# A hybrid encoder block on one core: squares on ScalarE, sums and the sine's product on VectorE, a third weight piece split early, new durations in the list

## The chip, the cores and the metric

The kernel runs on one core of a Trainium2 chip. The metric is the device time of one execution in microseconds, as the median of several executions. A core has five engines with a queue of instructions each, worked off in order: PE (TensorE, matmuls and transposes), DVE (VectorE), ACT (ScalarE), POOL (GpSimd) and SP (SyncE, which here only issues transfers). They wait for one another by semaphores. Data lie in DRAM, in SBUF (128 partitions) and in PSUM, where matmuls write.

## What is computed

One layer of an encoder with two kinds of heads, on a prompt of 512 rows and a sample of 256 rows, of width 2048, with shared weights. The reference, cut:

```
h = rmsnorm(x, ln_mix_g); z = h @ w_in            # 2048 -> 1024 fourier | 1024 q | 256 k | 256 v
of = fourier_mix(zf, w_fourier)                   # real part of a 2-D DFT per group of 128 channels, then 128x128
q, k = rope(q), rope(k)
s = q.k / 8, masked to |qpos - kpos| <= 128       # 16 heads, 4 kv heads, blocks of 128 queries
m = max(max(s), sink); p = exp(s - m)
p = p / (sum(p) + exp(sink - m)); oa = p @ v
x = x + concat(rmsnorm(of, g1), rmsnorm(oa, g2)) @ w_out
x = x + relu(rmsnorm(x, ln_mlp_g) @ w_up)**2 @ w_down   # 2048 -> 8192 -> 2048
y = rmsnorm(x, ln_final_g)
```

All is float32. A matmul that must keep that precision is made of three: both operands are split into a high and a low half in a shorter format, and high x high, high x low and low x high are summed.

## The kernel before, in words

The 768 rows are NM = 6 blocks m of 128 (0 to 3 prompt, 4 and 5 sample). The stages follow each other on PE: input projection (pz, L542, to 388 us), attention together with the Fourier half of the output projection (388 to 611 us), the attention half of the output projection (611 to 768 us), up-projection (pu, L1034, to 1693 us) and down-projection (pd, L1315, to 2590 us).

**Weight pieces.** A weight is loaded in pieces of 512 KB (`wload`, two raw buffers), and each piece is split: high half on ACT (L168), low half on DVE (L182), into one of four buffers `wh` and `wl`. The output projection has 32 pieces i: half 0 (Fourier rows) and half 1 (attention rows), in each four column strips n of 512, four pieces per strip. Pieces of half 1 carry a gain (L166 on ACT, L177 on DVE, two instructions each). The input projection is a loop of 36 pieces; callables put down with `after(piece, fn)` are run behind a piece, or in the middle of it (at piece - 0.5). So the first pieces of the output projection are loaded and split under the last input pieces.

**Attention.** There are 24 units u, one for each block b of 128 queries and each kv head g (four heads each). Blocks at the ends see 2 blocks of keys, those between see 3. A unit's steps: load the rotated, split queries (`load_q`, SP); for g = 3 instead load unrotated ones and rotate here (`rotate_q`: the product with the sine on POOL, L488; with the cosine on DVE, L490; their sum on DVE, L492; split on ACT L497 and DVE L500); scores s on PE (L584); maxima on DVE (L595, then L606 and L609); exponentials on ACT (L619, L614); row sum and its reciprocal on DVE (L625, L626); the normaliser p <- p * rs on POOL (L630, four steps, one for each head); transposes t of p on PE (L638, four per block of keys, each needs all heads' normalised p of its rows); their split into th (ACT, L644) and tl (DVE, L647); products with v on PE (o, L655); `take` copies o on ACT (L662); `put` stores its two halves by SP (L668).

**Fourier half of the output projection.** 24 slots (n, m) of 8 steps with three matmuls (pm, L739); a step needs its piece's low half. ACT takes a slot's result (xc, L752), SP stores it (y1, L755). These matmuls are what PE has to do while a unit's chain runs through the other engines.

**Attention's output.** When the four units of a block m are stored, SP loads it back (`oa_load`, L686) and POOL adds the second half in an accumulating load (L688). ACT and DVE split it (`oa_part`, L696 and L698), then `oa_square` squares both halves in place (L705) and adds them (L707), on POOL, and DVE sums over channels (`oa_reduce`, L712, into sr).

**The order of all this** is not left to a scheduler. Each step is a job: engine, assumed duration, due time, the jobs it needs, and a time `wait` behind its end until its result can be used. `in_turn(hop, slack)` plays the list through: it takes again and again the job that can start first on its engine (among equals the one due first), and the starting times give the order in which the code is emitted, which is the order in each engine's queue. A result is usable at end + wait + hop; for a job on PE other than a pm step, `slack` is added, so transposes, scores and products with v are put that much behind the assumed moment at which they could run, and pm steps fill the place.

**Attention half of the output projection.** For each strip n and each pair of blocks (mp, mp + 3): SP loads rows of x into yp (L943), POOL adds the stored first half in an accumulating load (L944), 8 steps of 6 matmuls run (pm, L739), for n = 0 the sums sr give the factor r (power on POOL, L99), DVE forms r * pm + yp (L962), and the result is stored. Its transposes (`x1_transpose`, ptx, L132) are made later, in step 3 of the next pair's matmuls; DVE and ACT turn them into factors for the up-projection.

Of the kernel before, what the change touches and what calls it, by code (L numbers as in the profile page):

```python
# [14 lines left out]
AF = mybir.ActivationFunctionType  # L15
ALU = mybir.AluOpType
# [24 lines left out]
def hybrid_encoder(ctx: ExitStack, tc: tile.TileContext, a: dict):  # L41
# [150 lines left out]
    with ExitStack() as ph:  # L192
# [292 lines left out]
        def rotate_q(u, step):  # L485
            x, y = state[u]["x"], state[u]["y"]
            if step == 0:
                nc.gpsimd.tensor_tensor(out=y, in0=y, in1=table(u, "sinr"), op=ALU.mult)  # L488
            elif step == 1:
                nc.vector.tensor_tensor(out=x, in0=x, in1=table(u, "cosr"), op=ALU.mult)  # L490
            else:
                nc.vector.tensor_tensor(out=x, in0=x, in1=y, op=ALU.add)  # L492
# [30 lines left out]
        for u in range(2):  # L523
            after(32.5 + u, lambda u=u: load_q(u))
        for i in range(2):
            after(32.5 + i, lambda i=i: (out_load(i), out_split(i)))
# [173 lines left out]
    def oa_square(m, step):  # L700

        x, y = oar[m, 0], oar[m, 1]
        if step < 2:
            z = (x, y)[step]
            nc.gpsimd.tensor_tensor(out=z[:], in0=z[:], in1=z[:], op=ALU.mult)  # L705
        else:
            nc.gpsimd.tensor_tensor(out=y[:], in0=y[:], in1=x[:], op=ALU.add)  # L707

# [88 lines left out]

    for i in range(2, 22):
        half, n, j = out_seq[i]
# [21 lines left out]
    for u in range(len(units)):  # L821
# [4 lines left out]
        if u >= 2:  # L826
            job(("q", u), SP, 0.5, t0 - 8, lambda u=u: load_q(u), ("s", u - 3, 3), ("<", ("q", u - 1)), start=8 if g == 3 else -1e9, wait=4.5)
        if g == 3:
            job(("r0", u), POOL, 1.2, t0 - 6, lambda u=u: rotate_q(u, 0), ("q", u))
            job(("r1", u), DVE, 0.62, t0 - 6, lambda u=u: rotate_q(u, 1), ("q", u))  # L830
            job(("r2", u), DVE, 0.62, t0 - 5, lambda u=u: rotate_q(u, 2), ("r0", u), ("r1", u))
            job(("q0", u), ACT, 0.56, t0 - 4, lambda u=u: split_q(u, 0), ("r2", u))
            job(("q1", u), DVE, 0.75, t0 - 3, lambda u=u: split_q(u, 1), ("q0", u))
# [21 lines left out]
        for h in range(4):  # L855
            job(("n", u, h), POOL, 0.6 if wide else 0.48, t0 + 5, lambda u=u, h=h: normalize(u, h), ("rs", u))
        for kb in range(nb):
# [14 lines left out]
        job(("o", u), ACT, 0.5, t0 + 11, lambda u=u: take(u), ("pv", u, nb - 1), ("put", u - 2))  # L872
        job(("put", u), SP, 0.5, t0 + 12, lambda u=u: put(u), ("o", u), wait=4)

    for m in range(NM):
        due = SLOT * (18 + m) + 4
        job(("a0", m), SP, 1.6, due, lambda m=m: oa_load(m, 0), *(("put", 4 * m + g) for g in range(4)), ("or", m - 2), wait=4)
        job(("a1", m), POOL, 2.4, due, lambda m=m: oa_load(m, 1), ("a0", m), wait=6)
        for i in range(2):
            job(("ph", m, i), ACT, 0.62, due + 5, lambda m=m, i=i: oa_part(m, i, 0), ("a1", m), ("mm", 3, m - 1, 7), ("ph", m, i - 1))  # L880
            job(("pl", m, i), DVE, 0.65, due + 6, lambda m=m, i=i: oa_part(m, i, 1), ("ph", m, i))
        for i in range(3):
            job(("sq", m, i), POOL, 1.2, due + 9, lambda m=m, i=i: oa_square(m, i), *(("pl", m, x) for x in ((i,) if i < 2 else (0, 1))), ("sq", m, i - 1))
        job(("or", m), DVE, 1.0, due + 12, lambda m=m: oa_reduce(m), ("sq", m, 2))

    with tc.manual_schedule(engines=by_hand):
        for key in in_turn(0.05, 0.4):
            jobs[key][3]()
# [41 lines left out]
    with tc.tile_pool(name="pp4", bufs=1, space=PSUM, reuse_waits="tile") as pp:  # L930
        pending, half = [], 0
        for n in range(4):
# [4 lines left out]
            for mp in range(3):  # L937
# [10 lines left out]
                def step(k):  # L948
                    if k == 3 and pending:
                        pt = pp.tile([P, 2, 512], F32, tag="pt", name="ptx", bufs=1)  # L950
                        x1_transpose(pt, *pending[0])
                        x1_factors(pt, *pending.pop(0)[:2])
# [569 lines left out]
```

## Time and profile before

| | before |
|---|---|
| median of 3 runs | 2618.87 us (2618.65 to 2619.86) |
| profiled execution | 2620.49 us |
| span of the profile | 2618.7 us |
| mean granted clock of TensorE | 0.998 |
| PE busy | 2588.1 us (99%) |
| DVE busy | 1700.7 us (65%) |
| ACT busy | 1042.4 us (40%) |
| POOL busy | 270.5 us (10%) |

The span runs from the first to the last instruction; the profiled execution's own time is 1.8 us longer. A row of the timeline has the start, the duration, the engine, the line, the operation with its names (out <- in), the shape, and how often; in square brackets stands how long the engine was idle before and what released it. A group (of the view by lines) gives count, busy time and mean duration in ns, then the idle time ahead and its releasers. A row of waits has the waiting instruction, what it waited for, the total, the number and the longest. A row of the chain has start, duration, what ran. A row of windows gives the stretch, its length, the busy time of PE, PEld (weight loads), DVE, ACT and POOL with counts, the granted clock, the DMA engines' share and GB/s.

### The profile page before, as it was taken

How to read it: one execution, taken by the hardware profiler on the slowest of the kernel's cores; microseconds unless marked ns; L12 is line 12 of the kernel's file. 1: busy time of each engine (PE TensorE's matmuls, PEld its weight loads, DVE VectorE, ACT ScalarE, POOL GpSimd, SP SyncE). 2: the span in 40 equal slices, each digit the busy share in tenths (PEclk: the TensorE clock that was granted, in tenths of full speed). 3: DMA queues.
4: the chain of work that ended last, by engine and by line, in shares of the span. 5: the costliest groups of instructions: out<-in, count | busy, mean ns of one | idle time of the engine just before them, and what ended most of it. 6: DMA issues, size and time to landing. Idle time of an engine off the chain costs nothing.

```text
span 2618.7 us, 34937 instructions
## 1 busy us (share of the span) xinstructions
PE 2588.1 (99%) x13556; PEld 2364.2 (90%) x13556; DVE 1700.7 (65%) x2073; ACT 1042.4 (40%) x1494; POOL 270.5 (10%) x381
## 2 busy tenths in 40 slices
PE   8999999999999999999999999999999999999998
PEld 8999997887889999999999999988888888888886
DVE  4344546665655655555777787767776765777677
ACT  6233316663333333333454445433333333333335
POOL 1011213434110111000000000020000000000000
PEclk9999999999999999999999999999999999999999
DMA  8333577547774554448666666585553672555364
GB/s 295 115 117 127 163 233 207 150 131 184 203 233 143 171 182 160 176 169 305 209 221 218 219 229 221 195 350 179 179 162 110 210 241 81 177 177 162 99 209 147
DMA packets 278982, 488.23 MB, mean 186 GB/s; under 512 B 21216, under 2 KB 171488, under 8 KB 277792
## 3 DMA queue, kind: packets, MB, share of 16 engines
q1 hardware_dynamic: 202240, 329.91, 39.2%
q10 hardware_dynamic: 54576, 96.58, 9.6%
q0 software_dynamic: 22000, 59.52, 8.2%
q8 instruction: 106, 1.74, 0.3%
q14 instruction: 60, 0.49, 0.1%
HBM read 359.30 MB, written 126.62 MB: 186 GB/s over the span
## 4 chain that ended last, share of the span: by engine, by line
PE 95%; DVE 2%; POOL 1%; ACT 1%; issue 1%; DMA 1%; ACTq 0%; POOLq 0%; SPq 0%; DVEq 0%
PE pu L1034 36%; PE pd L1315 34%; PE pz L542 11%; PE pm L739 8%; PE pv L222 1%; PE o L655 1%; PE s L584 1%; PE t L638 1%; PE pa L359 1%; PE pe L380 0%; PE ptx L132 0%; POOL p L630 0%; DVE wl L182 0%; DMA yp<-in_x_sample 0%; DMA raw<-in_w_out 0%
## 5 line engine op out<-in xcount | busy, mean ns | idle before, releaser
L1034 PE MATMUL pu<-xf,wh 128*128 128x384 f32 x3328 | 848.4, 336 | 0.0
L1034 PEld LDWEIGHTS pu<-xf,wh 128*128 128x128 f32 x3328 | 600.7, 188 | 1.9 <-ACT o L1052 1.1
L1034 PE MATMUL pu<-xf,wl 128*128 128x384 f32 x1664 | 559.1, 336 | 0.0
L1315 PE MATMUL pd<-wh,sh 128*128 128x512 f32 x1320 | 513.5, 389 | 0.0
L1315 PE MATMUL pd<-wl,sh 128*128 128x512 f32 x1320 | 513.5, 389 | 0.0
L1315 PE MATMUL pd<-wh,sl 128*128 128x512 f32 x1320 | 513.5, 389 | 0.0
L1292 ACT ACTIVATE wh<-rd 128x1024 fp32r<-128x1024 f32 x200 | 202.3, 1054 | 524.0 <-PE pd L1315 416.7
L1302 DVE TENSOR_TENSOR wl<-rd,wh 128x1024 fp32r<-128x1024 f32 x200 | 236.3, 1222 | 230.4 <-ACT wh L1292 229.7
L1014 ACT ACTIVATE wh<-ur 128x1024 fp32r<-128x1024 f32 x160 | 169.9, 1062 | 374.6 <-PE pu L1034 207.7
L1034 PEld LDWEIGHTS pu<-xf,wl 128*128 128x128 f32 x1664 | 312.8, 188 | 0.0
L1315 PEld LDWEIGHTS pd<-wl,sh 128*128 128x128 f32 x1320 | 247.8, 188 | 51.6
L1315 PEld LDWEIGHTS pd<-wh,sh 128*128 128x128 f32 x1320 | 247.7, 188 | 51.4
L1315 PEld LDWEIGHTS pd<-wh,sl 128*128 128x128 f32 x1320 | 247.7, 188 | 51.3
L1020 DVE TENSOR_TENSOR wl<-ur,wh 128x1024 fp32r<-128x1024 f32 x160 | 195.6, 1223 | 81.1 <-ACT wh L1014 81.1
L1055 DVE TENSOR_TENSOR o<-pu,o 128x768 f32<-128x768 f32 x160 | 153.0, 956 | 118.4 <-PE pu L1034 114.7
L542 PE MATMUL pz<-hh,wh 128*128 128x384 f32 x576 | 147.3, 336 | 0.0
L542 PE MATMUL pz<-hh,wl 128*128 128x384 f32 x576 | 146.3, 334 | 0.0
L542 PE MATMUL pz<-hl,wh 128*128 128x384 f32 x576 | 146.1, 334 | 0.0
L1285 DVE TENSOR_TENSOR rd<-rd 128x1024 f32<-128x1024 f32 x112 | 131.9, 1220 | 0.0
L1014 ACT ACTIVATE wh<-sx 128x1024 fp32r<-128x1024 f32 x64 | 67.9, 1062 | 127.7 <-PE pu L1034 96.7
L1305 DVE TENSOR_TENSOR sl<-sr,sh 128x768 fp32r<-128x768 f32 x110 | 104.7, 952 | 0.0
L542 PEld LDWEIGHTS pz<-hh,wl 128*128 128x128 f32 x576 | 103.9, 188 | 0.3 <-DVE wl L68 0.3
(210 smaller groups left out, 3489.1 us busy)
## 6 DMA issues: line engine op xcount, KB each, us to landing
rd<-in_w_down SPq DMA_DIRECT2D x176, 512.0 KB, 5.3
ur<-in_w_up SPq DMA_DIRECT2D x128, 512.0 KB, 3.9
sr<-sd SPq DMA_DIRECT2D x94, 384.0 KB, 5.5
pd<-o ACTq DMA_DIRECT2D x64, 384.0 KB, 2.3
o<-pd POOLq DMA_DIRECT2D x64, 384.0 KB, 6.1
sd<-sm ACTq DMA_DIRECT2D x60, 384.0 KB, 2.7
raw<-in_w_in SPq DMA_DIRECT2D x36, 512.0 KB, 3.6
raw<-in_w_out SPq DMA_DIRECT2D x32, 512.0 KB, 5.0
```

Of the source, the lines that this page charges most:

```text
L222: nc.tensor.matmul(pv[m][:, :256], l[j][:, i, m * P : (m + 1) * P], wv[j][r][:, i, :], start=(k == 0 and n == 0), stop=(k == NK - 1 and n ...
L542: nc.tensor.matmul(ps[c][s][:, :HALF], w[:, i, cs], h[j][:, i, s * HALF : (s + 1) * HALF], start=first and n == 0, stop=last and n == 2,)
L739: nc.tensor.matmul(ps[:], l(k), w[:, k % 2, :], start=(k == 0 and n == 0), stop=(k == 7 and n == 2))
L1014: nc.scalar.activation(wh[:], raw[:], AF.Copy)
L1020: nc.vector.tensor_tensor(out=wl[:], in0=raw[:], in1=f32(wh[:]), op=ALU.subtract)
L1034: nc.tensor.matmul(ps[:, t, :HALF], w[:, i, t * P : (t + 1) * P], xb[:, o, i, :], start=(s == first_of[bank] and i == 0 and n == 0), stop= ...
L1055: nc.vector.tensor_tensor(out=o, in0=src, in1=o, op=ALU.add)
L1285: add = lambda x, y, op: nc.vector.tensor_tensor(out=x[:], in0=x[:], in1=y[:], op=op)
L1292: nc.scalar.activation(wh[:], t[:], AF.Copy)
L1302: nc.vector.tensor_tensor(out=wl[:], in0=t[:], in1=f32(wh[:]), op=ALU.subtract)
L1305: nc.vector.tensor_tensor(out=sl[:], in0=sr[:], in1=f32(sh[:]), op=ALU.subtract)
L1315: nc.tensor.matmul(ps[m][:, ns], l[:, q, ts], w[:, ns], start=(j == 0 and q == 0 and t == 0), stop=(j == HP // 2 - 1 and q == 1 and t == 2),)
```

## The change

Six edits. The sine's product goes from POOL to DVE. The third piece of the output weight (i = 2) is loaded and split under the last input piece, not by the list. The two squares go from POOL to ACT, their sum to DVE. In the list, durations are set anew (query loads and stores 0.5 to 1.2, accumulating loads 2.4 to 3.6, the moved steps as on their new engines) and the first unit's normaliser gets a wait of 1.2. The slack of PE's jobs other than pm goes from 0.4 to 1.0. And the transposes of the pairs of strip n = 0 in the second half are made in step 6 of the next pair, not in step 3.

```
--- before.py
+++ after.py
@@ -485,7 +485,7 @@
         def rotate_q(u, step):
             x, y = state[u]["x"], state[u]["y"]
             if step == 0:
-                nc.gpsimd.tensor_tensor(out=y, in0=y, in1=table(u, "sinr"), op=ALU.mult)
+                nc.vector.tensor_tensor(out=y, in0=y, in1=table(u, "sinr"), op=ALU.mult)
             elif step == 1:
                 nc.vector.tensor_tensor(out=x, in0=x, in1=table(u, "cosr"), op=ALU.mult)
             else:
@@ -522,7 +522,7 @@
             after(23 + i // 2 if i < 4 else 25 + (i - 4) * 10 // 12 if i < 12 else 32 + (i - 12), fn)
         for u in range(2):
             after(32.5 + u, lambda u=u: load_q(u))
-        for i in range(2):
+        for i in range(3):
             after(32.5 + i, lambda i=i: (out_load(i), out_split(i)))
         for m in range(NM):
             after(0.5 + m // 2 * 0.5, lambda m=m: row_scale(m))
@@ -702,9 +702,9 @@
         x, y = oar[m, 0], oar[m, 1]
         if step < 2:
             z = (x, y)[step]
-            nc.gpsimd.tensor_tensor(out=z[:], in0=z[:], in1=z[:], op=ALU.mult)
+            nc.scalar.activation(z[:], z[:], AF.Square)
         else:
-            nc.gpsimd.tensor_tensor(out=y[:], in0=y[:], in1=x[:], op=ALU.add)
+            nc.vector.tensor_tensor(out=y[:], in0=y[:], in1=x[:], op=ALU.add)
 
     def oa_reduce(m):
 
@@ -795,7 +795,7 @@
     for m in range(NM):
         job(("of", m), SP, 3.0, SLOT * m - 20, lambda m=m: load_of(m), start=-22 if m < 2 else SLOT * m - 20, wait=4)
 
-    for i in range(2, 22):
+    for i in range(3, 22):
         half, n, j = out_seq[i]
         need = 6 * SLOT * (n + 4 * half) + 1.4 * j
         last = ("mm", out_seq[i - 4][1], NM - 1, 2 * out_seq[i - 4][2] + 1) if i >= 4 else None
@@ -824,9 +824,9 @@
         wide = nb == 3
         heads = [(h,) for h in range(4)] if wide else [(0, 1), (2, 3)]
         if u >= 2:
-            job(("q", u), SP, 0.5, t0 - 8, lambda u=u: load_q(u), ("s", u - 3, 3), ("<", ("q", u - 1)), start=8 if g == 3 else -1e9, wait=4.5)
+            job(("q", u), SP, 1.2, t0 - 8, lambda u=u: load_q(u), ("s", u - 3, 3), ("<", ("q", u - 1)), start=8 if g == 3 else -1e9, wait=4.5)
         if g == 3:
-            job(("r0", u), POOL, 1.2, t0 - 6, lambda u=u: rotate_q(u, 0), ("q", u))
+            job(("r0", u), DVE, 0.62, t0 - 6, lambda u=u: rotate_q(u, 0), ("q", u))
             job(("r1", u), DVE, 0.62, t0 - 6, lambda u=u: rotate_q(u, 1), ("q", u))
             job(("r2", u), DVE, 0.62, t0 - 5, lambda u=u: rotate_q(u, 2), ("r0", u), ("r1", u))
             job(("q0", u), ACT, 0.56, t0 - 4, lambda u=u: split_q(u, 0), ("r2", u))
@@ -853,7 +853,7 @@
             )
         job(("rs", u), DVE, 0.28, t0 + 5, lambda u=u: row_sum(u), *(("e", u, h) for h in range(5)))
         for h in range(4):
-            job(("n", u, h), POOL, 0.6 if wide else 0.48, t0 + 5, lambda u=u, h=h: normalize(u, h), ("rs", u))
+            job(("n", u, h), POOL, 0.6 if wide else 0.48, t0 + 5, lambda u=u, h=h: normalize(u, h), ("rs", u), wait=0.1 if u else 1.2)
         for kb in range(nb):
             one = turns[-1] if turns else (-1, 0)
             two = turns[-2] if len(turns) > 1 else (-1, 0)
@@ -870,21 +870,21 @@
                 ("l", u, kb), ("pv", u, kb - 1), ("o", u - 1), wait=0.2,
             )
         job(("o", u), ACT, 0.5, t0 + 11, lambda u=u: take(u), ("pv", u, nb - 1), ("put", u - 2))
-        job(("put", u), SP, 0.5, t0 + 12, lambda u=u: put(u), ("o", u), wait=4)
+        job(("put", u), SP, 1.2, t0 + 12, lambda u=u: put(u), ("o", u), wait=4)
 
     for m in range(NM):
         due = SLOT * (18 + m) + 4
         job(("a0", m), SP, 1.6, due, lambda m=m: oa_load(m, 0), *(("put", 4 * m + g) for g in range(4)), ("or", m - 2), wait=4)
-        job(("a1", m), POOL, 2.4, due, lambda m=m: oa_load(m, 1), ("a0", m), wait=6)
+        job(("a1", m), POOL, 3.6, due, lambda m=m: oa_load(m, 1), ("a0", m), wait=6)
         for i in range(2):
             job(("ph", m, i), ACT, 0.62, due + 5, lambda m=m, i=i: oa_part(m, i, 0), ("a1", m), ("mm", 3, m - 1, 7), ("ph", m, i - 1))
             job(("pl", m, i), DVE, 0.65, due + 6, lambda m=m, i=i: oa_part(m, i, 1), ("ph", m, i))
         for i in range(3):
-            job(("sq", m, i), POOL, 1.2, due + 9, lambda m=m, i=i: oa_square(m, i), *(("pl", m, x) for x in ((i,) if i < 2 else (0, 1))), ("sq", m, i - 1))
+            job(("sq", m, i), DVE if i == 2 else ACT, 0.68, due + 9, lambda m=m, i=i: oa_square(m, i), *(("pl", m, x) for x in ((i,) if i < 2 else (0, 1))), ("sq", m, i - 1))
         job(("or", m), DVE, 1.0, due + 12, lambda m=m: oa_reduce(m), ("sq", m, 2))
 
     with tc.manual_schedule(engines=by_hand):
-        for key in in_turn(0.05, 0.4):
+        for key in in_turn(0.05, 1.0):
             jobs[key][3]()
     att.close()
     kctx.close()
@@ -946,7 +946,7 @@
                     outs.append((ps, lambda k, m=m: oa[m][0][:, k, :], lambda k, m=m: oa[m][1][:, k, :]))
 
                 def step(k):
-                    if k == 3 and pending:
+                    if pending and k == (6 if pending[0][0] == 0 else 3):
                         pt = pp.tile([P, 2, 512], F32, tag="pt", name="ptx", bufs=1)
                         x1_transpose(pt, *pending[0])
                         x1_factors(pt, *pending.pop(0)[:2])
```

What moves by it, at three places. First DVE at the end of the input projection and the start of attention. L68 is the split of an input piece, L182 the low half of an output piece, L554 takes a finished result of the input projection (zs), L595 is a row maximum of unit 0 and then of unit 1 (one instruction and the reading of its result). A row with + stands in the kernel after, with - in the one before:

```order
 L427 TENSOR_TENSOR rx<-rx,ry 128x384
+L68 TENSOR_TENSOR wl<-raw,wh 128x1024
 L71 SCALAR_TENSOR_TENSOR rl<-rx,rh 128x384
-L68 TENSOR_TENSOR wl<-raw,wh 128x1024
+L182 TENSOR_TENSOR wl<-raw,wh 128x1024
 L554 TENSOR_TENSOR zs<-pz,rb 128x384 x4
+L595 ISA s,mx<-s,mask,sink 128x256
+L595 ISA mx 128x1
```

The third piece's low half now stands ahead of the last results of the input projection, and unit 0's first maxima (three, of which the first is shown) stand ahead of the fourth piece's low half instead of behind it.

Second DVE at unit 3's rotation, after only. L647 splits unit 0's transposes, L488, L490, L492 and L500 are unit 3's rotation and split, L625 and L626 are unit 1's row sum:

```order
+L647 TENSOR_TENSOR tl<-t,th 128x512 x2
+L488 TENSOR_TENSOR ry<-ry,sinr 64x512
+L490 TENSOR_TENSOR rx<-rx,cosr 64x512
+L625 TENSOR_TENSOR rs<-rs,es 128x4
+L626 RECIPROCAL rs<-rs 128x4
+L492 TENSOR_TENSOR rx<-rx,ry 64x512
+L500 SCALAR_TENSOR_TENSOR qs<-rx,qs 64x512
```

The sine's product, which waits for a load, now has unit 1's row sum behind it in DVE's queue; on POOL it had a normaliser behind it.

Third POOL through the first three blocks. L630 is the normaliser, L688 an accumulating load of a block of attention's output, L705 and L707 squares and sum:

```order
-L630 TENSOR_SCALAR p<-p,rs 128x256 x4
-L488 TENSOR_TENSOR ry<-ry,sinr 64x512
-L630 TENSOR_SCALAR p<-p,rs 128x256 x12
+L630 TENSOR_SCALAR p<-p,rs 128x256 x16
 L630 TENSOR_SCALAR p<-p,rs 128x384 x4
-L488 TENSOR_TENSOR ry<-ry,sinr 64x512
 L688 DMA oar<-oadl_93 128x4x128 x2
-L630 TENSOR_SCALAR p<-p,rs 128x384 x8
-L705 TENSOR_TENSOR oar<-oar 128x512 x2
-L707 TENSOR_TENSOR oar<-oar 128x512
```

POOL's queue keeps the normaliser and the accumulating loads. Further on, the third block's accumulating load moves from ahead of unit 14's normaliser to behind it. On PE, 27 pm matmuls follow unit 0's scores in both kernels; then come four of unit 1's score matmuls and unit 0's first transposes before, and all eight of unit 1's scores, three more pm matmuls and then the transposes after.

More of the change, by code (lines that the diff above doesn't have):

```diff
@@ L487, in rotate_q @@
             if step == 0:
-                nc.gpsimd.tensor_tensor(out=y, in0=y, in1=table(u, "sinr"), op=ALU.mult)
+                nc.vector.tensor_tensor(out=y, in0=y, in1=table(u, "sinr"), op=ALU.mult)
             elif step == 1:
@@ L524, in hybrid_encoder @@
             after(32.5 + u, lambda u=u: load_q(u))
-        for i in range(2):
+        for i in range(3):
             after(32.5 + i, lambda i=i: (out_load(i), out_split(i)))
@@ L704, in oa_square @@
             z = (x, y)[step]
-            nc.gpsimd.tensor_tensor(out=z[:], in0=z[:], in1=z[:], op=ALU.mult)
+            nc.scalar.activation(z[:], z[:], AF.Square)
         else:
-            nc.gpsimd.tensor_tensor(out=y[:], in0=y[:], in1=x[:], op=ALU.add)
+            nc.vector.tensor_tensor(out=y[:], in0=y[:], in1=x[:], op=ALU.add)
     def oa_reduce(m):
@@ L796, in hybrid_encoder @@
         job(("of", m), SP, 3.0, SLOT * m - 20, lambda m=m: load_of(m), start=-22 if m < 2 else SLOT * m - 20, wait=4)
-    for i in range(2, 22):
+    for i in range(3, 22):
         half, n, j = out_seq[i]
@@ L826, in hybrid_encoder @@
         if u >= 2:
-            job(("q", u), SP, 0.5, t0 - 8, lambda u=u: load_q(u), ("s", u - 3, 3), ("<", ("q", u - 1)), start=8 if g == 3 else -1e9, wait=4.5)
+            job(("q", u), SP, 1.2, t0 - 8, lambda u=u: load_q(u), ("s", u - 3, 3), ("<", ("q", u - 1)), start=8 if g == 3 else -1e9, wait=4.5)
         if g == 3:
-            job(("r0", u), POOL, 1.2, t0 - 6, lambda u=u: rotate_q(u, 0), ("q", u))
+            job(("r0", u), DVE, 0.62, t0 - 6, lambda u=u: rotate_q(u, 0), ("q", u))
             job(("r1", u), DVE, 0.62, t0 - 6, lambda u=u: rotate_q(u, 1), ("q", u))
@@ L855, in hybrid_encoder @@
         for h in range(4):
-            job(("n", u, h), POOL, 0.6 if wide else 0.48, t0 + 5, lambda u=u, h=h: normalize(u, h), ("rs", u))
+            job(("n", u, h), POOL, 0.6 if wide else 0.48, t0 + 5, lambda u=u, h=h: normalize(u, h), ("rs", u), wait=0.1 if u else 1.2)
         for kb in range(nb):
@@ L872, in hybrid_encoder @@
         job(("o", u), ACT, 0.5, t0 + 11, lambda u=u: take(u), ("pv", u, nb - 1), ("put", u - 2))
-        job(("put", u), SP, 0.5, t0 + 12, lambda u=u: put(u), ("o", u), wait=4)
+        job(("put", u), SP, 1.2, t0 + 12, lambda u=u: put(u), ("o", u), wait=4)
     for m in range(NM):
@@ L877, in hybrid_encoder @@
         job(("a0", m), SP, 1.6, due, lambda m=m: oa_load(m, 0), *(("put", 4 * m + g) for g in range(4)), ("or", m - 2), wait=4)
-        job(("a1", m), POOL, 2.4, due, lambda m=m: oa_load(m, 1), ("a0", m), wait=6)
+        job(("a1", m), POOL, 3.6, due, lambda m=m: oa_load(m, 1), ("a0", m), wait=6)
         for i in range(2):
@@ L882, in hybrid_encoder @@
         for i in range(3):
-            job(("sq", m, i), POOL, 1.2, due + 9, lambda m=m, i=i: oa_square(m, i), *(("pl", m, x) for x in ((i,) if i < 2 else (0, 1))), ("sq", m, i - 1))
+            job(("sq", m, i), DVE if i == 2 else ACT, 0.68, due + 9, lambda m=m, i=i: oa_square(m, i), *(("pl", m, x) for x in ((i,) if i < 2 else (0, 1))), ("sq", m, i - 1))
         job(("or", m), DVE, 1.0, due + 12, lambda m=m: oa_reduce(m), ("sq", m, 2))
     with tc.manual_schedule(engines=by_hand):
-        for key in in_turn(0.05, 0.4):
+        for key in in_turn(0.05, 1.0):
             jobs[key][3]()
@@ L948, in step @@
                 def step(k):
-                    if k == 3 and pending:
+                    if pending and k == (6 if pending[0][0] == 0 else 3):
                         pt = pp.tile([P, 2, 512], F32, tag="pt", name="ptx", bufs=1)
```

## The prediction

> **What bounds the kernel now.** I read the page first, then PE's waits from 385 to 640 us, then PE's timeline, the chain and the windows at the places that these named.
>
> ```profile
> PE 2588.1 (99%) x13556; PEld 2364.2 (90%) x13556; DVE 1700.7 (65%) x2073; ACT 1042.4 (40%) x1494; POOL 270.5 (10%) x381
> ```
>
> TensorE is busy for 99% of the span, and the change takes no matmul away. So all that it can win is time in which PE waits or runs slowly. Nearly all of that lies in the attention stage (388 to 611 us) and in the first slots of the attention half of the out-projection (611 to 640 us). The view of PE's waits there, with the total, the number and the longest:
>
> ```profile
> PE ptx L132 <- DVE yp L962: 2.8, 1, 2.8
> PE t L638 <- POOL p L630: 1.9, 3, 1.0
> PE pm L739 <- DVE wl L177: 1.5, 1, 1.5
> PE pm L739 <- DVE wl L182: 1.5, 2, 0.8
> PE o L655 <- DVE tl L647: 0.6, 1, 0.6
> PE s L584 <- ACT p L619: 0.4, 1, 0.4
> PE pm L739 <- ACT wh L168: 0.3, 1, 0.3
> ```
>
> They sum to 9.0 us, and this counts too little in two ways. A matmul's modelled end lies behind the next one's usual start, so each wait costs about 0.16 us more than its idle figure. And a group of eight transposes that is paced by the normaliser, block by block, shows as busy. PE's timeline, the first stalls and a healthy group of eight:
>
> ```profile
> 394.21 0.50 PE L739 MATMUL pm<-wl,ofh 128*128 128x512 f32 x1 [0.73 <-DVE wl L182]
> 397.84 2.13 PE L638 MATMUL t<-ident,p 128*128 128x128 f32 x8 [1.01 <-POOL p L630]
> 409.25 1.04 PE L638 MATMUL t<-ident,p 128*128 128x128 f32 x8
> ```
>
> I therefore took the losses from PE's starts: each interval less the usual one of its kind (pm 0.23 us, one transpose 0.11, a score of 256 columns 0.12). That gives three sums: start 4.9 us (waits 3.2, and 1.7 by the clock, below), middle 8.3, tail 4.85.
>
> The clock. Behind that first stall six matmuls of one line take 2.56 us by the chain, where the same six take 1.38 later; the window (us, busy PE, PEld, DVE, ACT, POOL, then the granted clock, DMA share, GB/s) shows why:
>
> ```profile
> 400.78 2.56 PE pm L739 x6
> 410.28 1.38 PE pm L739 x6
> ```
>
> ```profile
> 400.00:403.00 3.00, 3.00 (x10) 2.52 (x10) 2.32 (x7) 1.06 (x4) 0.00 (x0) 0.50 1.07 266
> ```
>
> The clock stood at 0.50 for 3.4 us, which costs 1.7.
>
> **The start: third weight piece split early, and the list's order.** Once the in-projection ends, ACT and DVE split pieces three and four one after the other, and the row maxima stand behind them. DVE, ACT, POOL:
>
> ```profile
> 390.40 1.23 DVE L182 TENSOR_TENSOR wl<-raw,wh 128x1024 fp32r<-128x1024 f32 x1 [1.55 <-ACT wh L168]
> 392.94 1.22 DVE L182 TENSOR_TENSOR wl<-raw,wh 128x1024 fp32r<-128x1024 f32 x1
> ```
>
> ```profile
> 391.62 1.06 ACT L168 ACTIVATE wh<-raw 128x1024 fp32r<-128x1024 f32 x1 [1.26 <-DMA raw<-in_w_out]
> ```
>
> ```profile
> 397.31 1.84 POOL L630 TENSOR_SCALAR p<-p,rs 128x256 f32<-128x256 f32 x4 [20.66 <-ACT xc L752]
> ```
>
> With the third piece done under the in-projection (its load is issued right behind the last input weight, its buffers are those of an earlier input piece), the fourth takes the third's place: low half done at 390.40 + 1.22, about 391.6. PE needs it at 394.21 less the stall of 0.89, that is 393.3, so this wait goes. Three of unit 0's maxima now come ahead of the fourth piece, so DVE's path to the row sums loses 1.23 + 1.22 and small gaps, 2.54 in my replay with these durations; the normaliser begins at 397.31 - 2.54 = 394.8 and its four steps of 0.46 end at 396.6. PE now has eight scores and three matmuls more where four scores stood, and comes to the first transposes at 397.0: no wait, by 0.4. Transposes done at 397.9 instead of 399.7, with 4 x 0.12 + 3 x 0.23 = 1.16 of other work done besides: 3.0 us. If the cover fails, it fails by the fourth piece's load (it was waited for, 1.26, in the row above) and costs at most the old 3.2. The clock's 1.7 I let go with the stall that it follows, for the profile; the profiled run is 2620.49 against a median of 2618.87, 1.62 more, so the timed runs may not have it. Start: 4.7 against the profile, 3.0 to 4.9.
>
> By the Trainium skill, "TensorE: Matmul & The Clock Gate", section "HAM oscillation — how this bites in real kernels", a slowed clock follows a gap in PE's work of more than about 3.4 us; here the gaps ahead of it are 0.73 and 1.01 us, so the row disagrees, and by that rule alone the 1.7 would come from something that this change does not touch: 3.0 for the start.
>
> **The middle: products and squares off POOL.** The stalls, one for each kind, and what POOL did ahead of the first:
>
> ```profile
> 517.55 2.63 POOL L688 DMA_DIRECT2D oar<-oadl  x2 [6.76 <-DMA oar<-oadh]
> ```
>
> ```profile
> 520.75 2.09 PE L638 MATMUL t<-ident,p 128*128 128x128 f32 x8 [0.51 <-POOL p L630]
> 566.25 1.39 PE L638 MATMUL t<-ident,p 128*128 128x128 f32 x8
> 570.55 0.50 PE L739 MATMUL pm<-wl,ofh 128*128 128x512 f32 x1 [0.76 <-DVE wl L182]
> 583.38 2.04 PE L638 MATMUL t<-ident,p 128*128 128x128 f32 x8
> 593.74 1.88 PE L638 MATMUL t<-ident,p 128*128 128x128 f32 x8
> ```
>
> Against a healthy 1.04 these groups lose 1.05 + 0.35 + 1.00 + 0.84, with the idle 0.51 and 0.76 before them 4.5; the other 3.8 of the 8.3 are the 0.16s and places below 0.7 each. Operations before, by group (busy, mean ns, idle before and its releaser):
>
> ```profile
> L705 POOL TENSOR_TENSOR oar<-oar 128x512 f32<-128x512 f32 x12 | 14.2, 1189 | 16.7 <-DVE oal L698 15.9 <-ACT xc L752 0.8
> L698 DVE TENSOR_TENSOR oal<-oar,oah 128x512 fp32r<-128x512 f32 x12 | 9.8, 827 | 1.7 <-ACT oah L696 1.6
> L707 POOL TENSOR_TENSOR oar<-oar 128x512 f32<-128x512 f32 x6 | 9.8, 1626 | 0.2
> L488 POOL TENSOR_TENSOR ry<-ry,sinr 64x512 f32<-64x512 f32 x6 | 8.6, 1438 | 13.7 <-DMA ry<-zq 13.7
> L696 ACT ACTIVATE oah<-oar 128x512 fp32r<-128x512 f32 x12 | 7.6, 634 | 2.8 <-DMA oar<-oadl 2.8
> L492 DVE TENSOR_TENSOR rx<-rx,ry 64x512 f32<-64x512 f32 x6 | 4.1, 684 | 4.8 <-POOL ry L488 4.7
> ```
>
> POOL gives up 14.2 + 9.8 + 8.6 = 32.6 us and keeps the normaliser, the accumulating loads and four small powers. ACT takes 12 squares: no row shows one of this shape beside its copy, 0.63, which is the nearest; 12 x 0.63 = 7.6. DVE takes 6 products (0.68 by the row of the same shape; up to the 1.44 of POOL) and 6 sums (0.83; 0.68 to 1.63): 4.1 + 5.0 = 9.1, between 8.2 and 18.4. DVE's load near the third boundary of the weights is the cost:
>
> ```profile
> 559.00:568.00 9.00, 8.87 (x48) 7.34 (x47) 8.68 (x24) 6.34 (x17) 4.12 (x5) 1.00 0.58 178
> ```
>
> DVE has 0.3 us to spare there, and a product of 0.68 comes on top. Some of it is paid back at once, since POOL's product and DVE's were in each other's way:
>
> ```profile
> 560.54 1.99 POOL L488 TENSOR_TENSOR ry<-ry,sinr 64x512 f32<-64x512 f32 x1 [4.52 <-DMA ry<-zq]
> ```
>
> ```profile
> 561.29 1.78 DVE L490 TENSOR_TENSOR rx<-rx,cosr 64x512 f32<-64x512 f32 x1
> ```
>
> 1.78 against 0.68: the moved product costs DVE 0.68 and frees 1.1 where they overlapped. Where a stall goes, what is late next? With POOL free and the slack of the list's transposes and scores at 1.0, the normaliser has 7 to 10 us from a unit's last score to its first transpose, where the path through maxima, exponentials and four normalising steps took 5.2 to 6.5 undisturbed; unit 14's accumulating load (2.63) now stands behind its normaliser. So units 14, 20 and 22 lose their 1.0 to 1.7. What my replay leaves is DVE's: two weight pieces at each boundary of n, 0.9 at the first, 0.75 at the second, 1.9 at the third as before, and 0.3 in unit 1, 3.85 in all (from none to the old 8.3). PE changes between kinds of matmul 251 times instead of 244, 0.06 each: 0.4. Middle: 8.3 - 3.85 - 0.4 = 4.0, from 0 to 7.9. The longer durations of loads and stores in the list (q, put, a1) only move SP's and POOL's issues, which have idle time there; they cost nothing while a load still leads its user, and 2.6 us of POOL where one does not, as in the 517.55 row.
>
> **The tail.** First slots of the second half; PE, DVE, POOL and a window:
>
> ```profile
> 618.92 0.50 PE L739 MATMUL pm<-wl,oah 128*128 128x512 f32 x1 [1.54 <-DVE wl L177]
> 633.40 1.22 PE L132 MATMUL ptx<-ident,yp 128*128 128x128 f32 x8 [2.78 <-DVE yp L962]
> ```
>
> ```profile
> 617.17 1.03 DVE L712 TENSOR_REDUCE sr<-oar 128x128 f32<-128x512 f32 x1 [2.52 <-POOL oar L707]
> 618.12 1.41 DVE L177 SCALAR_TENSOR_TENSOR wl<-raw,gains,wh 128x512 fp32r<-128x512 f32 x2
> ```
>
> ```profile
> 631.02 0.85 POOL L944 DMA_DIRECT2D yp<-y  x1 [4.67 <-DMA yp<-in_x_sample]
> ```
>
> ```profile
> 613.00:622.00 9.00, 7.46 (x33) 5.61 (x32) 5.92 (x8) 3.83 (x6) 5.59 (x6) 1.00 1.14 267
> ```
>
> The split for PE's first stall stands behind a sum that DVE awaits from POOL for 2.52 us. With squares on ACT and the add on DVE, that wait is 0.63 + 0.83 of work instead of two POOL steps, and the split is ready before its user: the 1.54 (1.8 with restart) goes to about 0.3. The second stall is a chain: raw buffer free, load, yp load landing, accumulate at 631.02, power, DVE, transposes. Its load is issued some 1.4 us earlier, as the split ahead of it is, and for n = 0 the transposes move behind 18 more matmuls, 18 x 0.23 = 4.1 us: by 2.94 + 0.1 of stall less 4.1 it goes, if the loads keep step with a stage that comes 7 to 9 us earlier; 0.6 is left at the stage's fourth piece. Tail: 4.85 - 0.9 = 3.95, from 0 to 4.85.
>
> **The sum.** 4.7 + 4.0 + 3.95 = 12.65 against the profiled execution's 2620.49: 2607.8. Against the median, 11.0 (no clock) to 12.65: 2606.2 to 2607.9. I take 2607.5. The rest of the kernel (up and down projection) shows no wait of PE that any edit touches.
>
> **The rivals.**
> 1. Slower: DVE's queue becomes the bound. The product now stands in DVE's queue, and there it waits for its load with row sums of another unit behind it (unit 1's, at unit 3's rotation). POOL waited 13.7 us for these loads (the L488 row); if DVE inherits the wait with 4.1 + 5.0 of new work, all uncovered, it is 22.8 less 12.65: 10.2 above the profile, about 2629. It decides from 12.65 / 22.8 = 55% uncovered. Against it: with the third piece's load early, the loads of unit 3 go out ahead of their old time, and at most places the row maxima are what stands next.
> 2. The weight boundaries eat the middle: DVE at 8.68 of 9.00 says so for one of three. The start and the tail alone are 8.65, or 7.0 without the clock: 2610 to 2612, say 2611.
> 3. The tail is bound by transfers: share 1.14 and 267 GB/s in the last window. Then the 3.95 does not come, and what the last units win (after 583: about 2.6) is only waited for: 12.65 - 6.55 = 6.1, or 4.4 without the clock, some 2613.8.
> 4. DVE's new operations hold the normaliser up, as the pair at 560.54 and 561.29 held each other. Twelve operations of 0.7 on a normaliser's path: 8.4 of the 12.65 go, 4.2 are left, 2614.5. Against it: POOL's 24 operations of that kind are gone at the same time. By the Trainium skill, "SBUF — State Buffer", section "Who interferes with whom", a VectorE operation with both inputs in SBUF shares a port with a GpSimd one that reads SBUF, and whoever comes second waits out the whole instruction; the pair agrees.
>
> **The chances.** Forecast 0.62 (its own range 2603 to 2611.5), rival 1 0.05, 2 0.17, 3 0.09, 4 0.07. The low end takes the middle at 7 and the tail at its bound, 2603; the high end takes in rivals 2, 3 and half of 4: 2614.5. A measurement of this kernel tells about 0.2%, 5.2 us, so faster means below 2613.6: the forecast, most of rival 2 and a third of 3, 0.81; same 0.14; slower 0.05.
>
> **What would show it.** Right: no wait of t on p at the first unit, clock 1.00 at 400 us, groups of eight at 1.04 for units 14, 20 and 22, no stall of PE at the second ptx. Wrong: waits of t on p that end with DVE's product behind a load (rival 1), pm on wl at n = 1 and 2 (rival 2), ptx still waiting for yp (rival 3), normalising steps above 0.46 beside DVE's sums (rival 4).

## The result and the profile after

The kernel after takes 2613.14 us (median of 10 runs, 2611.61 to 2614.71); the kernel before, 10 runs beside it, 2620.14. The ratio is 0.9975, interval 0.9966 to 0.9983: 7.0 us faster, where 11.4 were forecast (2607.5 from 2618.87). The profiled execution took 2613.02 us, its span is 2611.2.

The page's row of engines and PE's waits from 380 to 640 us, after:

```profile
PE 2584.0 (99%) x13556; PEld 2363.5 (91%) x13556; DVE 1702.9 (65%) x2085; ACT 1048.1 (40%) x1506; POOL 245.2 (9%) x357
```

```profile
PE pm L739 <- ACT wh L166: 2.3, 1, 2.3
PE pm L739 <- DVE wl L182: 2.1, 4, 0.8
PE pz L542 <- DVE wl L68: 0.9, 1, 0.9
PE pm L739 <- DVE wl L177: 0.3, 1, 0.3
PE t L638 <- POOL p L630: 0.2, 1, 0.2
```

The waits of t on p and of ptx on yp are as good as gone. New is the first row: 2.3 us on the high half of a piece with a gain, that is in the second half's first slots.

To see where time went I cut every trace at the same three instructions of PE: the first score (L584), the first matmul of the second half (pm from oah), the first of the up-projection (L1034; it stands at 758.7 us in the kernel before, not at the 768 of the account ahead). "Attention" is the first stretch, "tail" the second. Beside them stands what PE lost by the prediction's method (intervals between starts, less the usual one, where over 0.06 us), in attention's first 27 us, the rest of attention, and the tail; every kernel of this study is in it, from its one profiled execution:

| kernel | ratio to before, interval | attention | tail | lost: start | middle | tail |
|---|---|---|---|---|---|---|
| before | 1 | 223.75 | 147.15 | 5.2 | 11.3 | 6.3 |
| after | 0.9975 (0.9966 to 0.9983) | 215.35 | 148.33 | 2.5 | 6.1 | 7.6 |
| after_again | 0.9975 (0.9964 to 0.9986) | 216.07 | 147.79 | 2.7 | 6.6 | 7.0 |
| tail_order | 0.9965 (0.9952 to 0.9977) | 216.15 | 144.93 | 3.3 | 6.1 | 4.1 |
| tail_and_first_ptx | 0.9967 (0.9954 to 0.9980) | 215.78 | 145.56 | 2.7 | 6.2 | 4.6 |
| undo_slack | 0.9994 (0.9985 to 1.0003) | 224.58 | 145.71 | 3.7 | 13.7 | 5.0 |
| undo_squares | 0.9986 (0.9977 to 0.9994) | 218.97 | 150.47 | 2.6 | 9.4 | 9.5 |
| undo_third_piece | 0.9984 (0.9975 to 0.9993) | 218.07 | 148.88 | 4.6 | 6.6 | 8.2 |
| undo_ptx_step | 0.9983 (0.9974 to 0.9992) | 214.76 | 149.95 | 2.1 | 5.9 | 9.1 |
| undo_product | 0.9971 (0.9960 to 0.9982) | 216.14 | 147.25 | 2.9 | 6.4 | 6.5 |
| undo_durations | 0.9968 (0.9956 to 0.9981) | 216.19 | 147.42 | 2.6 | 6.7 | 6.7 |
| only_slack | 0.9997 (0.9988 to 1.0006) | 220.11 | 148.61 | 3.2 | 10.0 | 7.9 |
| only_squares | 0.9984 (0.9975 to 0.9993) | 220.81 | 146.39 | 4.6 | 9.0 | 5.7 |
| slack_squares | 0.9997 (0.9988 to 1.0005) | 223.51 | 148.05 | 7.4 | 9.3 | 7.2 |

These losses also hold the changes between kinds of matmul and the half clock, so they are larger than the sums of the prediction; they are compared among themselves. Kernels that share attention's steps with the kernel after lie between 214.8 and 216.2 there, which is how far one profile can be trusted. The profiled execution of only_slack was the fastest of its eleven (2616.85, median 2620.70) and that of only_squares the slowest (2620.04, median 2615.70), so these two rows and their ratios don't match.

Attention became 7.7 to 8.4 us shorter; the tail, where 3.95 were to be won, 0.6 to 1.2 longer. Together that is 7.0 to 7.2 us, the measured gain.

**Start.** ACT, DVE, POOL and PE after the change:

```profile
391.51 1.06 ACT L168 ACTIVATE wh<-raw 128x1024 fp32r<-128x1024 f32 x1 [9.65 <-DMA raw<-in_w_out]
```

```profile
392.61 1.23 DVE L182 TENSOR_TENSOR wl<-raw,wh 128x1024 fp32r<-128x1024 f32 x1 [2.46 <-ACT wh L168]
```

```profile
396.98 1.84 POOL L630 TENSOR_SCALAR p<-p,rs 128x256 f32<-128x256 f32 x4 [18.85 <-PE s L584]
```

```profile
393.89 0.50 PE L739 MATMUL pm<-wl,ofh 128*128 128x512 f32 x1 [0.55 <-DVE wl L182]
397.52 2.12 PE L638 MATMUL t<-ident,p 128*128 128x128 f32 x8
```

The fourth piece's split did not take the third's place: ACT was idle 9.65 us and waited for its load until 391.5, as before (391.62). The load went out only 1.0 us earlier, at 383.58 instead of 384.56, and took longer, 7.85 us against about 6.8; why, was not followed. So its low half is ready 0.3 us earlier, not 2.5, unit 0's fourth maximum still stands behind it, and the normaliser begins at 396.98 instead of 397.31. PE has no wait ahead of its first transposes because it has 1.16 us more of other work, but the group is still paced by the normaliser, 2.12 against 1.04. The clock after it stayed at 1.00 (400 to 403 us).

**Middle.** Three groups of transposes of units that stalled before, and the moved operations by group:

```profile
515.74 1.04 PE L638 MATMUL t<-ident,p 128*128 128x128 f32 x8
```

```profile
560.53 1.42 PE L638 MATMUL t<-ident,p 128*128 128x128 f32 x8
586.84 1.03 PE L638 MATMUL t<-ident,p 128*128 128x128 f32 x8
```

```profile
L698 DVE TENSOR_TENSOR oal<-oar,oah 128x512 fp32r<-128x512 f32 x12 | 8.0, 684 | 5.5 <-ACT oah L696 5.5
L705 ACT ACTIVATE oar<-oar 128x512 f32<-128x512 f32 x12 | 7.3, 637 | 1.4 <-DVE oal L698 0.9 <-DVE rs L625 0.5
L707 DVE TENSOR_TENSOR oar<-oar 128x512 f32<-128x512 f32 x6 | 5.5, 915 | 4.0 <-ACT oar L705 4.0
L488 DVE TENSOR_TENSOR ry<-ry,sinr 64x512 f32<-64x512 f32 x6 | 4.1, 678 | 0.5 <-DMA ry<-zq 0.5
```

Counted along PE's transposes these are units 14, 20 and 23, which took 2.09, 1.39 and 1.88 before; unit 22 came from 2.04 to 1.08. So 14, 22 and 23 run free now, and unit 20 is paced as it was. Costs came as estimated: a square 0.637 (0.63), a product 0.678 (0.68), a sum 0.915 (0.83). The product waited 0.5 us in all for its loads on DVE, where POOL had waited 13.7.

**Tail.** PE, ACT and DVE, then the end of the chain of waits:

```profile
610.88 0.49 PE L739 MATMUL pm<-wh,oah 128*128 128x512 f32 x1 [2.27 <-ACT wh L166]
611.67 0.59 PE L739 MATMUL pm<-wl,oah 128*128 128x512 f32 x1 [0.29 <-DVE wl L177]
```

```profile
599.15 1.14 ACT L705 ACTIVATE oar<-oar 128x512 f32<-128x512 f32 x2
600.20 2.55 ACT L166 ACTIVATE wh<-raw,gains 128x512 fp32r<-128x512 f32 x4
...
610.10 2.60 ACT L166 ACTIVATE wh<-raw,gains 128x512 fp32r<-128x512 f32 x4 [6.21 <-DMA raw<-in_w_out]
```

```profile
600.33 0.69 DVE L707 TENSOR_TENSOR oar<-oar 128x512 f32<-128x512 f32 x1 [0.92 <-ACT oar L705]
601.05 1.09 DVE L712 TENSOR_REDUCE sr<-oar 128x128 f32<-128x512 f32 x1
602.07 2.72 DVE L177 SCALAR_TENSOR_TENSOR wl<-raw,gains,wh 128x512 fp32r<-128x512 f32 x4
```

```profile
603.49 6.59 DMA raw<-in_w_out
610.08 0.02 issue
610.10 0.73 ACT wh L166
```

Read upwards from PE: piece 18's split waits for its load, the load for a raw buffer (603.49), the buffer for the low half of piece 16 (two steps from 602.07 on), and this for DVE's sum and reduction of block 4's squares; on ACT the high half of piece 16 stands behind the two squares themselves. In the kernel before, this load went out at 609.87, 1.7 us ahead of the second half's first matmul (611.55), and took 4.2 us; here it goes out 0.5 us behind that matmul (603.00) and takes 6.59. So against PE it is 2.2 us late by the queues and 2.4 by the transfer. A window over the stretch behind PE's wait shows the price besides:

```profile
612.00:615.00 3.00, 3.00 (x8) 2.32 (x7) 2.80 (x5) 2.51 (x6) 1.76 (x2) 0.50 0.55 158
```

### The profile page after: what moved, and what is told of

The parts are those of the page before. It is cut to its first block, busy times and chain, and to the rows that moved or that the text cites. A ratio compares the mean times of both kernels' runs of the same rounds, so it can differ in the third digit from the quotient of the medians.

```text
span 2611.2 us, 34913 instructions
## 1 busy us (share of the span) xinstructions
PE 2584.0 (99%) x13556; PEld 2363.5 (91%) x13556; DVE 1702.9 (65%) x2085; ACT 1048.1 (40%) x1506; POOL 245.2 (9%) x357
## 4 chain that ended last, share of the span: by engine, by line
PE 80%; DMA 3%; DVE 2%; ACT 1%; issue 1%; POOL 0%; SPq 0%; ACTq 0%; POOLq 0%; DVEq 0%
PE pu L1034 36%; PE pd L1315 34%; PE pm L739 7%; DMA raw<-in_w_out 1%; DMA qh<-rh 1%; PE s L584 1%; PE o L655 1%; PE t L638 1%; DMA ry<-zq 0%; DMA zq<-zs 0%; PE ptx L132 0%; DVE wl L182 0%; DMA oar<-oadl 0%; DVE wl L177 0%; DVE acc L1249 0%
## 5 line engine op out<-in xcount | busy, mean ns | idle before, releaser
L1034 PE MATMUL pu<-xf,wh 128*128 128x384 f32 x3328 | 848.7, 336 | 0.0
L1034 PEld LDWEIGHTS pu<-xf,wh 128*128 128x128 f32 x3328 | 600.5, 188 | 1.7 <-ACT o L1052 1.2
L1034 PE MATMUL pu<-xf,wl 128*128 128x384 f32 x1664 | 559.1, 336 | 0.0
L1034 PEld LDWEIGHTS pu<-xf,wl 128*128 128x128 f32 x1664 | 312.8, 188 | 0.0
```

The lines of the kernel that those rows point to most:

```text
L1034: nc.tensor.matmul(ps[:, t, :HALF], w[:, i, t * P : (t + 1) * P], xb[:, o, i, :], start=(s == first_of[bank] and i == 0 and n == 0), stop= ...
```

## The experiments

My theory of the shortfall was this queue order; the rival, that the loads of the second half land when the transfer engines let them (rival 3 of the prediction). For attention the question was which edit made its gain.

**Splits of pieces 16 and 17 ahead of block 4's squares.** One more need in the list:

```
-*(("pl", m, x) for x in ((i,) if i < 2 else (0, 1))), ("sq", m, i - 1))
+*(("pl", m, x) for x in ((i,) if i < 2 else (0, 1))), ("sq", m, i - 1), ("lo", 17) if m == 4 else None)
```

> The kernel after, but block 4's squares and their sum are made to wait in the list for the splits of pieces 16 and 17, so ACT and DVE have those splits first; nothing else moves. Theory (queue order): in the kernel after the squares and the sum stand ahead of piece 16's split, the raw buffer comes free about 2.2 us later against PE, and with it the load of piece 18. So here PE's wait on the high half in the first slots of the second half goes from 2.3 to 0.5 or less, the second wait of 0.3 goes, and the half clock behind them (1.7) too: 4 to 4.5 us faster than the kernel after, near 2609 or a ratio of 0.996 to the kernel before. Rival (transfers): the load of piece 18 lands when the DMA engines let it, near 610 us whatever is queued on ACT; the wait stays above 1.5 us and the time near 2613.

Measured: 2611.40 us. ACT, SP and PE:

```profile
599.64 2.55 ACT L166 ACTIVATE wh<-raw,gains 128x512 fp32r<-128x512 f32 x4
602.10 1.14 ACT L705 ACTIVATE oar<-oar 128x512 f32<-128x512 f32 x2
...
607.24 1.34 ACT L166 ACTIVATE wh<-raw,gains 128x512 fp32r<-128x512 f32 x2 [3.08 <-DMA raw<-in_w_out]
```

```profile
601.83 1.70 SPq L77 DMA_DIRECT2D raw<-in_w_out  x2
```

```profile
612.10 0.50 PE L739 MATMUL pm<-wl,oah 128*128 128x512 f32 x1 [0.28 <-DVE wl L177]
```

The load goes out 1.7 us earlier and takes 5.4 us, its split starts at 607.24 instead of 610.10, the wait of 2.27 and the half clock are gone, and the tail is 2.9 to 3.4 us shorter than in the two profiles of the kernel after. The order in ACT's and DVE's queues is shown as the cause of this wait; that the load also took 1.2 us less leaves the transfers a share in it. By the ratios the gain is 0.0010 of the time, 2.6 us, with intervals that overlap. It is less than the 4 to 4.5 expected: the half clock does not follow the wait each time (last section), and two waits at the second strip, 0.67 and 0.41 in the kernel after, are 1.11 and 0.40 here.

**Later transposes for the first pair only.** In that kernel also `6 if pending[0][:2] == (0, 0) else 3`.

> The kernel of tail_order with the transposes of x1 late (step 6) only for the first pair, which is the one that waits for its load, and in step 3 for the other two of the first strip. Theory (the later factors of the last pair of the first strip stand ahead of the split of pieces 22 and 23): the two waits of PE on the low half at the second strip, 1.27 and 0.57 in tail_order and 0.8 and 0.6 in the kernel after, go, and no wait of ptx comes: 1 to 1.8 us faster than tail_order, 2609.5 to 2610.5. Rival (those waits come from the loads): they stay, and the time is that of tail_order.

Measured: 2610.83 us. PE:

```profile
626.24 1.22 PE L132 MATMUL ptx<-ident,yp 128*128 128x128 f32 x8 [0.18 <-DVE yp L962]
637.03 0.66 PE L132 MATMUL ptx<-ident,yp 128*128 128x128 f32 x4 [1.79 <-DVE yp L962]
```

The waits at the second strip went, as they do with step 6 undone (next run), so they did come from the later factors; the longer one lies between 0.57 (undo_slack) and 2.50 (undo_third_piece) in all kernels that have step 6 for the whole strip. But the second pair's transposes, which waited neither before nor in the kernel after, now wait 1.79. The theory's price was wrong: no gain over tail_order that can be told.

**Step 6 undone.** `if k == 3 and pending:` as before.

> The kernel after with the transposes of x1 in step 3 for all strips. Theory: the wait of ptx on yp comes back at the first pair, 2 us or more, but what the later step costs goes: the two waits on the low half at the second strip (0.8 and 0.6 with restarts), where the factors' work stands ahead of the split: 2613 to 2615. Rival (the prediction's step: the later step is gain alone): the wait of 2.8 to 3 us comes back and nothing goes: 2616 or more.

Measured: 2616.16 us, some 2 us slower than the kernel after by the ratios. PE and a window behind the wait:

```profile
626.27 1.67 PE L132 MATMUL ptx<-ident,yp 128*128 128x128 f32 x8 [3.65 <-DVE yp L962]
```

```profile
628.00:630.00 2.00, 2.00 (x6) 1.52 (x6) 1.90 (x4) 0.63 (x1) 0.00 (x0) 0.50 0.82 283
```

Theory and rival are both half right: a wait larger than in the kernel before returned, as the prediction's step has it, and the waits at the second strip went, as my theory had it. By the ratios the later step is worth some 2 us, with intervals that overlap.

**Slack back to 0.4.** `in_turn(0.05, 0.4)`.

> The kernel after with the slack of PE's jobs back at 0.4. Theory (slack made the start's gain and much of the middle's): four scores and three pm fewer ahead of the first transposes, the stall of about 1 us on p and the half clock behind it come back (2.9 us), and in the middle at least 2 us of waits of t on p or o on tl: 2617 to 2619. Rival (POOL relief made them): the middle keeps its 3.3 us of losses within 0.7, the start loses at most 1.2: 2613 to 2614.5.

Measured: 2619.02 us. PE's waits from 385 to 640 us:

```profile
PE t L638 <- POOL p L630: 4.6, 9, 0.9
PE pm L739 <- ACT wh L166: 1.4, 1, 1.4
```

All of attention's gain goes (224.58), by nine waits on the normaliser, with POOL as free as in the kernel after. At the start the theory was wrong: no wait of 1 us at the first transposes came back, the waits are at unit 1 and later.

**Squares and sum back on POOL**, with 1.2 each in the list.

> The kernel after with squares and sum back on POOL, in the code and in the list (1.2 each). Theory (POOL relief made the middle's gain): waits of t on p come back at the units whose normaliser stands behind squares, 2 to 4 us of the middle, and piece 18's wait in the tail goes or is replaced by DVE's wait on POOL's sum: 2612 to 2616. Rival (the list's slack made the middle's gain): no wait of t on p comes back above 0.3 us, the tail loses its wait of 2.3 and the half clock, and the time is 2609 to 2611.

Measured: 2616.57 us. PE's waits from 385 to 640 us:

```profile
PE pm L739 <- ACT wh L166: 1.8, 1, 1.8
PE pm L739 <- DVE wl L182: 1.5, 3, 0.8
PE t L638 <- POOL p L630: 1.4, 3, 0.6
```

Attention is about 3 us longer, as the theory had it. But the tail's wait on a high half did not go, and a half clock follows it; it is at the next piece, 19 (618.22), whose load waits for a split that stands behind DVE's wait of 2.52 us for POOL's sum. In only_slack, with the squares on POOL too, piece 19 costs a wait of 3.29. So the queue order shown above is the cause in the kernel after, not a general one.

**Third piece back in the list**, `range(2)` and the list from 2.

> The kernel after with two weight pieces split in the input projection instead of three, the list from piece 2. Theory: the early third piece gives nothing at the start, since the fourth piece's load lands at 391.5 us either way and unit 0's row sum came only 0.33 us earlier, and it costs the wait of 1.1 us that the last input piece has on its low half; without it 2612 to 2613, and the wait of pz on the low half is gone. Rival (the prediction's step): it was worth 2.5 us of the start, so the stall at the first transposes comes back with the half clock: 2615 to 2617.

Measured: 2616.51 us, by the ratios 2.4 us slower than the kernel after, with intervals that overlap. My theory falls; the time is the rival's, but not by the rival's stall, for there is no wait at the first transposes. The last input piece's wait did not go (1.1 and 0.3 us), and attention is 2.0 to 2.7 us longer; not at unit 0, as the prediction had it, but at unit 1, whose transposes now wait 0.5 and 0.6 with two paced groups behind them. That wait of pz is no work of the edit either: it was 0 in after_again, in undo_slack and in only_slack, and 2.3 with a half clock in only_squares, which has the old code there.

**Product back on POOL**, and, apart from it, **the durations of the list as before**.

> The kernel after with the sine's product back on POOL, in the code and in the list. Theory (the list's slack covers a short step ahead of the normaliser; what mattered were the squares): the stage from unit 0's first score to the up-projection takes 363.7 us in the kernel after and here stays within 1.5 us of that: 2612 to 2615. Rival (each of six products on POOL holds a normaliser back, as DVE's free queue let it pass): waits of t on p of 0.5 or more at units 3, 7, 11, 15, 19 or 23, 3 us or more in all: 2616 to 2618.

Measured: 2612.53 us.

> The kernel after with the list's durations of query loads, stores, accumulating loads and the first normaliser's wait as before. Theory (they move SP's and POOL's issues and little else): the stage takes 363.7 us within 1.5, 2612 to 2615. Rival (they place the third block's accumulating load behind unit 14's normaliser and give the first transposes their cover): a wait of t on p of 1 us or more at unit 0 or unit 14, with the half clock behind it or not: 2615 to 2618.

Measured: 2612.63 us. Neither can be told from the kernel after; both theories hold, and both rivals fall.

**Edits alone, on the kernel before**: the slack; the squares and sum; both.

> The kernel before with only the slack changed to 1.0. Theory (slack and the moves off POOL need each other, since the kernel after lost 3.4 us by the squares alone and 5.9 by the slack alone): 2616 to 2619, with waits of t on p left in the units that have squares ahead of the normaliser. Rival (the slack alone makes the gain, and the other edits are there for nothing): 2612.5 to 2615, no wait of t on p above 0.5 us past unit 1.

Measured: 2620.70 us.

> The kernel before with only the squares moved to ACT and their sum to DVE, in the code and in the list. Theory (slack and moved squares need each other; with a slack of 0.4 PE comes to the transposes before the path through maxima and exponentials ends, whoever squares): at most 2 us faster, 2618 to 2620.5, with waits of t on p all over the middle. Rival (the squares alone freed the normaliser): 2614 to 2617.

Measured: 2615.70 us.

> The kernel before with both the slack of 1.0 and the squares and sum moved; product, third piece, durations and the later transposes of x1 as before. Theory: the two together make the middle's gain, so 3 to 5 us below the kernel before, 2615 to 2617.5, and what is missing to the kernel after is the wait of ptx on yp (about 3) and the third piece. Rival (no pair: each edit has its own share, and these two have 0.3 and what only_squares shows): the sum of the two alone, 2618 or more.

Measured: 2619.19 us. PE at unit 1 and the window behind it:

```profile
408.25 0.33 PE L638 MATMUL t<-ident,p 128*128 128x128 f32 x1 [1.02 <-POOL p L630]
409.13 1.68 PE L638 MATMUL t<-ident,p 128*128 128x128 f32 x7 [0.55 <-POOL p L630]
```

```profile
411.00:414.00 3.00, 3.00 (x9) 2.35 (x8) 1.77 (x6) 2.52 (x11) 0.00 (x0) 0.50 0.92 281
```

I had expected a pair: little from each, 3 to 5 us from both. It came the other way round, and for the squares alone the rival was right: the squares alone gain 3.7 us, the slack alone nothing, and the two together nothing. Both together lose 4.3 us at unit 1, 1.7 of it by the half clock, and keep the tail's wait of ptx, 3.0. The third and the fourth piece are both split behind the in-projection there, but so they are in only_slack, which loses 0.2 at unit 1: why these two together stall there is open. In only_squares PE comes to the second half no earlier than before (612.02 against 611.55) and yet waits 2.02 us on piece 18's high half: the moved squares alone bring that wait; with the slack besides it is 0.39. So the edits don't add: each gives another order of the whole list, and what it wins in one place another place can take. Why the middle loses 9.3 us with these two and 6.6 with all but the third piece is not settled; undoing the product or the durations alone did not show it.

**The kernel after again.**

> The kernel after, unchanged, on this chip, for comparison with the one above: 0.9975 of the kernel before, as measured, give or take 0.0009. Theory and rival say the same here; what may differ is the start and the wait of the last input piece, which differed between kernels that share that code.

Measured: 2611.98 us, ratio 0.9975. As expected; the wait of the last input piece did not come.

## Why the prediction was right and where its size was off

- **The time:** 2613.14 lies in the whole range, 2603 to 2614.5, but above the forecast's own, which ended at 2611.5. The upper end had been set to take in rivals 2, 3 and half of 4; without that room the time would have been missed.
- **Bound by PE, gain only from its waits:** right. PE's busy time fell by 4.1 us without a matmul less, which is paced groups in the main: units 14, 22 and 23 make 2.9 of it. Each of the two profiles holds one stretch of half clock, so the clock does not explain it.
- **Start, 4.7:** losses fell from 5.2 to 2.5 and 2.7, so about 2.6, of which 1.7 is the clock: the waits gave 0.9 where 3.0 were counted. Nor is the 1.7 shown to be the change's work, since it hangs on where a stall falls (last section); only_slack waited 0.73 and 0.56 there without losing it. The step that failed is "the fourth takes the third's place": its load lands at 391.5 either way, and with it the path to the row sum (0.33 us earlier, not 2.54). The third piece paid at unit 1 instead: undone, 2.2 us are lost there, against 0.3.
- **Middle, 4.0:** losses fell by 4.7 to 5.2. Mechanism and size right, but for unit 20, which the prediction named among the groups that would run at 1.04 and which is at 1.42; the losses of 1.00 and 0.84 that it listed are those of units 22 and 23. Which edit makes it, the prediction gave to POOL's relief and the slack together. Undone singly, the slack takes back all, the squares some 3 us, the product and the durations nothing that can be told; slack and squares alone don't make the gain, and what else it needs is open.
- **Attention as a whole, 8.7:** 7.7 to 8.4. That this is near is in part luck, a start that was too short and a middle that was larger.
- **Tail, 3.95:** lost 0.6 to 1.2 instead. The step that failed is "the split is ready before its user". It is the split of piece 18, for whose low half PE waited 1.54 before. DVE no longer waits for POOL there, but the split now waits for its load. The squares and the sum moved to ACT and DVE came to stand ahead of piece 16's split there, which the prediction did not count as a cost of the move; with it the load of piece 18 went out late and took longer, while PE came 8.5 us earlier. The other half held: the later transposes don't wait, though their factors cost 0.67 and 0.41 at the second strip.
- **Rivals.** 1: the product waited 0.5 us on DVE; nothing of it. (Its 2629 is 10.2 above the median; above the profile it would be 2630.7.) 2: the boundary that stood at 564 to 570 kept its waits (0.41 and 0.34 us on the low half, 0.76 before), the middle as a whole did not. 3: the tail gave nothing, as this rival had it, but transfers have only a share in that: tail_order gave back 3 us with the same bytes. 4: the normaliser's steps of 128x256 took 627 ns on average, 623 before, and DVE's two-input steps became faster as POOL stopped reading beside them (L698 from 827 to 684 ns, the row above). The undone edits show it the other way: L698 is at 808 with the squares back on POOL, L490 at 906 with the product back, where the kernel after has 676. By the Trainium skill, "SBUF — State Buffer", section "Who interferes with whom", such a VectorE step contends with a GpSimd one that reads SBUF; the fall agrees.

## What to carry to other kernels

A step that is taken off a slack engine lands in two other queues: ask at every place what stands behind it there, above all the steps that free a buffer for the next load. Where a hand-made list orders all engines, edits to it don't add; measure them undone one at a time from the final version, not only alone. Before a stall is written off because its work comes earlier, look whether its load does.

## What was not expected of the hardware

The clock dropped to 0.50 for 3.4 us behind waits of PE shorter than that, and not always: behind 2.27 and 0.29 us in the kernel after, but not behind 2.33 and 0.29 in after_again, the same kernel; nor behind the single 2.78 of the kernel before. The waits in after_again:

```profile
611.58 0.49 PE L739 MATMUL pm<-wh,oah 128*128 128x512 f32 x1 [2.33 <-ACT wh L166]
612.37 0.50 PE L739 MATMUL pm<-wl,oah 128*128 128x512 f32 x1 [0.29 <-DVE wl L177]
```

The traces show what decides. Within each of the 14 traces, all changes of the granted clock lie whole multiples of 3.413 us apart: in the kernel after they come at 11.19, 611.93, 615.35 and 2601.90, which is 176, 1 and 582 steps. So one can lay this grid over a profile. The kernel after, then after_again, in steps of their own grids:

```profile
608.52:611.93 3.41, 0.84 (x3) 0.45 (x3) 1.07 (x2) 1.83 (x3) 0.00 (x0) 1.00 0.93 357
611.93:615.35 3.42, 3.42 (x9) 2.65 (x9) 2.87 (x5) 2.93 (x6) 1.76 (x2) 0.50 0.58 171
```

```profile
607.26:610.67 3.41, 1.99 (x9) 1.31 (x7) 0.00 (x0) 0.00 (x0) 0.00 (x0) 1.00 0.73 238
610.67:614.08 3.41, 2.21 (x8) 1.61 (x9) 2.52 (x4) 3.27 (x6) 0.21 (x1) 1.00 0.71 271
```

In the kernel after, both waits fall into one step: PE is idle for 2.57 of its 3.41 us, and the next step runs at half. In after_again a border of the grid cuts the wait in two, 1.42 and 1.20 us of idle, and the clock stays. The 2.78 of the kernel before was cut likewise, at 632.00. From 376 to 700 us, over all 14 traces, each of the eight steps with 1.96 us of idle or more is followed by a half clock, and no step with less is (the largest has 1.79), but for two that hold a group of paced transposes besides: 1.39 in the kernel before (396.48 to 399.90) and 1.70 in slack_squares (407.36 to 410.78).

So a wait of about 2 us costs 2 or 3.7 us, by where it falls on a grid whose position differs from execution to execution. That is likely part of why executions of one kernel spread by some 3 us here and a single profile can mislead: in the last group of runs, the kernel before took 2617.6 us on average where the mean clock of the execution was 0.999 (4 executions), 2619.4 at 0.998 (15) and 2622.8 at 0.997 (4).
